# A trunk layer's output projection: its row multiply, its loads and its stores go to other engines, and one value tile moves behind the state space output

## The chip, the cores and the metric

The kernel runs on one core of a Trainium2 chip. The metric is the device time of one execution in microseconds (us); the time of a version is the median of its runs. TensorE (PE) does the matrix products, VectorE (DVE), ScalarE (ACT) and GpSimd (POOL) the elementwise work. SyncE (SP) only asks for transfers; ACT and POOL can ask for them too. Each engine works through its own list of instructions in order: an instruction that waits holds up all that stand behind it on that engine.

## The reference, cut to what matters

```python
h = rms_norm(x, mix_pre_g)
proj = h @ w_in                          # columns: u | q | k | v | f_logit
y_ssm = s5_mixer(u, ...)                 # scan over time, gelu(y), times sigmoid(g @ glu_w + glu_b)
y_fox = forgetting_attention(q, k, v, f_logit + fox_f_bias)      # 8 heads of 64
y_mix = concatenate([rms_norm(y_ssm, ssm_out_g), rms_norm(y_fox, fox_out_g)], -1)
x = x + rms_norm(y_mix @ w_out, mix_post_g)                      # the output projection
x = x + rms_norm(memory_cross_attention(rms_norm(x, xa_pre_g), ...), xa_post_g)
x = x + rms_norm(swiglu(rms_norm(x, ffn_pre_g), ...), ffn_post_g)
```

There are 1024 tokens of 1024 float32 values. `x1` below is x after the first of the three sums.

## The kernel before, in words

**Products.** A float32 product is made of three: each operand is split into a high part, rounded by an ACT copy (line 113), and the low rest, by a DVE subtraction (line 115, or 117 with a gain). `mm3` (lines 121 to 124) then multiplies high by high, high by low and low by high.

**The order of work.** The program is written by a framework that lists the instructions in the order in which the source makes them, and then plans the lists of the engines with a simulated clock. Of the instructions that are ready it takes the one with the best priority, which is the place in the source, moved ahead by 5000 places inside `tc.high_priority(offset=boost)`. Buffers come from pools with a fixed count for each tag; a tile that finds none free waits until all readers of an older tile are done. The tags that matter here: `t2` (3 buffers), `a` (2), `b` (2), `c` (3), `d` and `e` (1 each), `slab` (16), `raw` (2), `whl` (3). In PSUM there are four banks `g`, and during attention two double banks `s`, later four banks `x`.

**Where v and the state space output meet.** `in_proj` (line 869) ends with `V1_AT`: it makes that many tiles of the second half of v (`v1`, eight tiles of 24 products each, one `g` bank each), then takes one step of `ssm_out`, and so on:

```python
V1_AT = (3, 1, 1, 1, 1)
for n in V1_AT:
    step(v1, n)
    step(go)
drain(go)
```

A step of `ssm_out` (line 635) is either the four batches `b` of one half (lines 643 and 644, one `g` bank each, followed by a Gelu on ACT, line 645, into the slab `go`) or the transposes of one quarter (line 655). A v tile is copied from its bank by ACT (line 316) into a `t2` buffer, and POOL stores it (line 319). Before that the q and k tiles store their high parts from `t2` buffers too (line 297). What is left of `v1` is made by `fillers` (line 975), the side work that is spread over the steps of the attention `fox`.

**The output projection.** `out_ssm` (line 818) has stored the half result of the state space columns in `t1_d`. After attention the loop at line 1057 adds the half of the attention columns, tile by tile of 128 tokens, in the order 3, 4, 5, 6, 7, 0, 1, 2 (called n = 0 to 7 here). For a tile SP asks for x (tag `c`, line 1060), then for the half result `t` in two transfers (tags `a`, `a`, `b` in turn, line 1063). For each half of the columns PE makes 12 products into an `x` bank; DVE adds them, scaled by `r_f`, to `t` (line 1070); ACT squares two quarters (line 1072); POOL multiplies the half by the row `g_mp`, the gain `mix_post_g` for all partitions (line 1074). Then DVE sums the squares (1076), `rsqrt_mean` makes `r` with two small ACT and three small DVE instructions (lines 137 to 145), DVE forms x1 in the tile of x (line 1078), and for n = 0 to 4 POOL stores it (line 1082). The row `g_mp` lies in the one `d` buffer, which holds the sum of squares of the attention until line 815.

After each half of the columns the loop takes one step of `first_values`: the products of the cross-attention's values with its output weights for heads 0 and 1 (`value_weights`, line 1033, with its operand `vh` in a buffer of tag `b`, `e`, `b`, `e` for heads 0 to 3). Heads 2 and 3 and the `a` operands (`build_a(1)`) follow the loop.

Of the kernel before, what the change touches and what calls it, by code (L numbers as in the profile page):

```python
# [10 lines left out]
F32R = mybir.dt.float32r  # L11
BF16 = mybir.dt.bfloat16
AF = mybir.ActivationFunctionType
ALU = mybir.AluOpType
# [3 lines left out]
P = 128  # L18
# [16 lines left out]
MAGIC = 12582912.0  # L35
RATE = 1.02
HP = 16 * (L - 1)
V1_AT = (3, 1, 1, 1, 1)
HID = ("11", "12", "22", "S1", "S2", "S3", "S4")
EVB = 13  # L40
OPB = 10
# [11 lines left out]
def layer(ctx: ExitStack, tc: tile.TileContext, a, out):  # L53
    nc = tc.nc
    dve, act, pool, pe, sp = nc.vector, nc.scalar, nc.gpsimd, nc.tensor, nc.sync
# [13 lines left out]
    def slab(shape, dt=F32R):  # L69
        return slabp.tile(shape, dt, name="slab", tag="slab")  # L70
# [13 lines left out]
    def sm(n, name):  # L84
        return small.tile([P, n], F32, name=name, tag=name)
# [26 lines left out]
    def split(hi, lo, src, mul=None, lo_eng=None):  # L112
        first = act.activation(out=hi, in_=src, func=AF.Copy, scale=1.0 if mul is None else mul)  # L113
        if mul is None:
            (lo_eng or dve).tensor_tensor(out=lo, in0=src, in1=hi.bitcast(F32), op=ALU.subtract)  # L115
        else:
            dve.scalar_tensor_tensor(out=lo, in0=src, scalar=mul, in1=hi.bitcast(F32),
                                     op0=ALU.mult, op1=ALU.subtract)
        return first

    def mm3(ps, lh, ll, rh, rl, first, last):
        pe.matmul(ps, lh, rh, start=first, stop=False)  # L122
        pe.matmul(ps, lh, rl, start=False, stop=False)  # L123
        pe.matmul(ps, ll, rh, start=False, stop=last)  # L124
# [23 lines left out]
    boost = 5000  # L148
    stA, stB, stC = pool, pool, pool
# [4 lines left out]
    def load_w(src, shape, first=0, stage=None):  # L154
        w = tt(stage, [P, D]) if stage else raw([P, D])
        hl = whl([P, 2, D])
        if not first:
            sp.dma_start(out=w, in_=src)
        for cs in (slice(0, first), slice(first, D)):
            if cs.start < cs.stop:  # L160
                if first:
                    sp.dma_start(out=w[:, cs], in_=src[:, cs])
                with tc.high_priority(offset=boost):
                    split(hl[:, 0, cs], hl[:, 1, cs], w[:, cs])
        v = hl.rearrange("p t (a b) -> p t a b", b=shape)
        return v[:, 0], v[:, 1]
# [16 lines left out]
    t1_d = dram.tile([L, NC, D], F32, name="t1_d")  # L183
    kv_d = dram.tile([16, P, 256], F32, name="kv_d")
    x1_d = dram.tile([NT, P, D], F32, name="x1_d")
# [9 lines left out]
    def tt(tag, shape=None, dt=F32):  # L195
        return t4.tile(shape or [P, S], dt, name=tag, tag=tag, bufs=BUFS[tag])

    def t2t(shape, dt=F32):
        return tt("t2", shape, dt)
# [435 lines left out]
    def ssm_out():  # L635
        U, T, SS, mo = ssm_made
        for s_ in range(2):
            go = slab([P, 2, L, P], F32)
            with tc.high_priority(offset=boost):
                for b in range(4):  # L640
                    ps = g_ps([P, 4, NC])
                    for g in range(4):
                        pe.matmul(ps[:, g], U[s_][:, 4 * b + g], T[s_][:, 4 * b + g], start=True, stop=False)
                        pe.matmul(ps[:, g], SS[s_][:, 4 * b + g], mo[s_][:, 4 * b + g], start=False, stop=True)
                    g_ = act.activation(out=go[:, b // 2].rearrange("c j (g i) -> c g j i", i=16)[:, 4 * (b % 2):4 * (b % 2) + 4],
                                        in_=ps.rearrange("c g (j i) -> c g j i", i=16), func=AF.Gelu_apprx_tanh)
                    if (s_, b) == (0, 3):
                        last.append(g_)
            yield
            for ft in range(2):  # L650
                hl = slab([P, 2, S])
                for b in range(2):
                    tp = g_ps([P, 4, NC])
                    for j in range(4):
                        pe.transpose(tp[:, j], go[:, ft, 4 * b + j], ident)
                    cs = slice(512 * b, 512 * b + 512)
                    split(hl[:, 0, cs], hl[:, 1, cs], tp.rearrange("p j c -> p (j c)"))
                gl.append(hl)
                yield
# [192 lines left out]
    def step(g, n=1):  # L852
        for _ in range(n):
            if next(g, "end") == "end":
                return
# [13 lines left out]
    def in_proj():  # L869
# [11 lines left out]
        go = ssm_out()  # L881
        for n in V1_AT:
            step(v1, n)
# [61 lines left out]
    def gain_row(i, tag):  # L945
        g = tt(tag)
        sp.dma_start(out=g, in_=a["post_g"][i:i + 1, :].broadcast_to([P, D]))
        return g
# [71 lines left out]
    def x_ps(shape):  # L1020
        return psx.tile(shape, F32, name="x", tag="x")

    wo = []
    for i in range(4):
        w = raw([P, D])
# [1 line left out]
        hl = slab([P, 2, D])  # L1027
        split(hl[:, 0], hl[:, 1], w)
        wo.append(hl)
    g_mp = gain_row(0, "d")  # L1030
    VW = {}

    def value_weights(h):
        vr = t2t([P, 2, 256])
        sp.dma_start(out=vr, in_=kv_d[8 + 2 * h:8 + 2 * h + 2].rearrange("d p m -> p d m"))
        vh = tt("bebe"[h], [P, 2, 2, 256], F32R)
        split(vh[:, 0], vh[:, 1], vr)
        wo_ = [load_w(a["wo"][2 * h + d], 512) for d in range(2)]
        for mt in range(2):
            VW[2 * h + mt] = slab([P, 2, D])  # L1040
        for c in range(2):
            tiles = [(mt, (x_ps if h == 3 else g_ps)([P, 512])) for mt in range(2)]
            for d in range(2):
                for mt, ps in tiles:
                    ms = slice(mt * P, mt * P + P)
                    mm3(ps, vh[:, 0, d, ms], vh[:, 1, d, ms], wo_[d][0][:, c], wo_[d][1][:, c], d == 0, d == 1)
                    yield
            for mt, ps in tiles:
                split(VW[2 * h + mt][:, 0, c * 512:c * 512 + 512], VW[2 * h + mt][:, 1, c * 512:c * 512 + 512], ps)

    def first_values():
        for h in range(2):
            yield from value_weights(h)
# [2 lines left out]
    kept = {}  # L1056
    for n, j in enumerate((3, 4, 5, 6, 7, 0, 1, 2)):
        ts = slice(j * P, (j + 1) * P)
        xt = tt("c")
        sp.dma_start(out=xt, in_=a["x"][ts, :])  # L1060
        t = tt("aab"[n % 3])
        for i in range(2):
            sp.dma_start(out=t[64 * i:64 * i + 64], in_=t1_d.rearrange("j (k s) d -> s k j d", s=16)[2 * j + i])
        ss4, ss, r = sm(4, "ss4"), sm(1, "ss"), sm(1, "r")
        for h in range(2):
            hs = slice(h * 512, h * 512 + 512)
            ps = x_ps([P, 512])
            for k in range(4):
                mm3(ps, yf[k][:, 0, ts], yf[k][:, 1, ts], wo[k][:, 0, hs], wo[k][:, 1, hs], k == 0, k == 3)
            dve.scalar_tensor_tensor(out=t[:, hs], in0=ps, scalar=r_f[:, j:j + 1], in1=t[:, hs], op0=ALU.mult, op1=ALU.add)  # L1070
            for q in range(2 * h, 2 * h + 2):
                act.activation(out=tt("yt", [P, 256]), in_=t[:, q * 256:q * 256 + 256], func=AF.Square,
                               accum_out=ss4[:, q:q + 1])
            pool.tensor_tensor(out=t[:, hs], in0=t[:, hs], in1=g_mp[:, hs], op=ALU.mult)
            step(between)
        dve.tensor_reduce(out=ss, in_=ss4, op=ALU.add, axis=mybir.AxisListType.X)
        rsqrt_mean(r, ss, D)
        dve.scalar_tensor_tensor(out=xt, in0=t, scalar=r, in1=xt, op0=ALU.mult, op1=ALU.add)
        if j < 3:
            kept[j] = xt  # L1080
        else:
            stC.dma_start(out=x1_d[j], in_=xt)


    drain(between)
# [144 lines left out]

    keys = build_a(1)
    drain(value_weights(2))
    step(keys, KT // 2)
    xa_prep(0)
    drain(value_weights(3))
    xa_turn(0)
    drain(keys)
# [391 lines left out]
```

## Time and profile before

| | us |
|---|---|
| median of 3 runs | 1414.27 (1410.5, 1414.27, 1419.89) |
| the profiled execution: its own time | 1414.33 |
| its span, first to last instruction | 1412.5 |
| PE busy in the span | 1381.8 |
| DVE busy | 951.9 |
| ACT busy | 652.3 |
| POOL busy | 379.7 |

1.83 us of the profiled execution lie outside its span. Attention ends and the output projection begins at about 490 us of the span; the loop of line 1057 ends at about 558 us. Busy times overlap. A PE row's duration overlaps with that of its successor, so the distance between starts tells the pace: about 0.23 us for a product of 512 columns and 0.12 us for one of 256 at full clock, twice that at half clock.

### The profile page before, as it was taken

The numbers are of one execution on the slowest core, as the hardware profiler recorded it, in microseconds if no ns is written. First come the engines' busy times: TensorE is split into PE (matmuls) and PEld (weight loads), VectorE is DVE, ScalarE is ACT, GpSimd is POOL, SyncE is SP. The second block draws the span as 40 slices with busy tenths as digits, with TensorE's granted clock in tenths as the row PEclk, the third lists the DMA queues.
The fourth block names the chain that finished last, engine by engine and source line by source line (L and its number), as shares of the span: only waits on it lengthen the run. The fifth ranks groups of instructions, "written<-read, shape, count | busy, mean of one in ns | idle before, by whom it ended". The sixth has DMA issues, their size and how long they took to land.

```text
span 1412.5 us, 20273 instructions
## 1 busy us (share of the span) xinstructions
PE 1381.8 (98%) x7353; PEld 1163.3 (82%) x7353; DVE 951.9 (67%) x1719; ACT 652.3 (46%) x1289; POOL 379.7 (27%) x430
## 2 busy tenths in 40 slices
PE   9999989999999899999999999999999999999997
PEld 7889889789889677888888788888888888888886
DVE  8949944857567668545467777877776676655566
ACT  7383345766566546433344533333333334544351
POOL 0011110011211043001021367676766661000021
PEclk9999999999999999999999999999999999999999
DMA  6235665267663665024467345554444447955544
GB/s 217 91 108 163 201 220 138 69 200 213 183 180 113 175 194 186 27 75 152 161 202 257 97 176 193 178 187 161 145 158 154 165 150 236 357 196 194 179 164 164
DMA packets 104501, 239.45 MB, mean 170 GB/s; under 512 B 11464, under 2 KB 40136, under 8 KB 104272
## 3 DMA queue, kind: packets, MB, share of 16 engines
q1 hardware_dynamic: 85872, 176.24, 40.0%
q0 software_dynamic: 18528, 61.91, 12.3%
q8 instruction: 58, 0.95, 0.3%
q14 instruction: 43, 0.35, 0.1%
HBM read 169.43 MB, written 77.33 MB: 175 GB/s over the span
## 4 chain that ended last, share of the span: by engine, by line
PE 84%; DVE 7%; issue 3%; DMA 3%; ACT 2%; POOL 0%; SPq 0%; DVEq 0%; ACTq 0%; POOLq 0%
PE x L1294 17%; PE g L1294 13%; PE x L1557 7%; PE g L1557 7%; PE g L122 7%; PE g L124 7%; PE g L123 7%; PE x L123 2%; PE x L124 2%; PE g L758 2%; PE x L122 2%; PE g L772 2%; PE s L730 1%; PE s L731 1%; DMA a<-t_d 1%
## 5 line engine op out<-in xcount | busy, mean ns | idle before, releaser
L1294 PE MATMUL x<-slab,op 128*128 128x512 f32 x984 | 233.2, 389 | 0.5 <-DVE op L115 0.5
L1294 PEld LDWEIGHTS x<-slab,op 128*128 128x128 f32 x984 | 184.7, 188 | 39.2 <-DVE op L115 1.0
L1294 PE MATMUL g<-slab,op 128*128 128x512 f32 x744 | 178.7, 389 | 0.0
L115 DVE TENSOR_TENSOR slab<-slab 128x1024 fp32r<-128x1024 f32 (+2 forms) x92 | 110.2, 1207 | 86.4 <-ACT slab L113 85.2
L1294 PEld LDWEIGHTS g<-slab,op 128*128 128x128 f32 x744 | 139.7, 188 | 29.0
L122 PE MATMUL g<-slab,whl 128*128 128x512 f32 (+1 forms) x416 | 151.4, 364 | 0.8 <-ACT slab L485 0.4
L124 PE MATMUL g<-slab,whl 128*128 128x512 f32 (+1 forms) x416 | 148.7, 358 | 0.0
L123 PE MATMUL g<-slab,whl 128*128 128x512 f32 (+1 forms) x416 | 148.3, 357 | 0.0
L113 ACT ACTIVATE slab<-slab 128x1024 fp32r<-128x1024 f32 (+2 forms) x92 | 94.7, 1036 | 108.6 <-DMA slab<-hs_d 80.8
L1557 PE MATMUL g<-slab 128*128 128x512 f32 x462 | 126.6, 389 | 0.0
L1557 PE MATMUL x<-slab 128*128 128x512 f32 x462 | 126.6, 389 | 0.0
L1557 PEld LDWEIGHTS g<-slab 128*128 128x128 f32 x462 | 86.7, 188 | 18.0
L1557 PEld LDWEIGHTS x<-slab 128*128 128x128 f32 x462 | 86.7, 188 | 18.0
L115 DVE TENSOR_TENSOR op<-slab,op 128x512 fp32r<-128x512 f32 x80 | 84.6, 1068 | 11.5 <-ACT op L113 11.3
L1370 POOL TENSOR_TENSOR wt<-wt 128x256 f32<-128x256 f32 x88 | 83.1, 944 | 21.0 <-DMA wt<-in_w_down 17.4
L122 PE MATMUL g<-whl,slab 128*128 128x256 f32 (+2 forms) x288 | 86.8, 310 | 1.7 <-ACT yt L318 0.7
L122 PEld LDWEIGHTS g<-slab,whl 128*128 128x128 f32 x416 | 78.6, 189 | 12.0 <-ACT whl L113 0.6
L124 PEld LDWEIGHTS g<-slab,whl 128*128 128x128 f32 x416 | 78.4, 189 | 11.6 <-DVE whl L115 0.2
L123 PEld LDWEIGHTS g<-slab,whl 128*128 128x128 f32 x416 | 78.6, 189 | 10.6
L113 ACT ACTIVATE op<-slab 128x512 fp32r<-128x512 f32 x80 | 50.0, 628 | 79.9 <-PE g L1294 38.0
L124 PE MATMUL g<-whl,slab 128*128 128x256 f32 (+2 forms) x288 | 86.0, 299 | 0.0
L123 PE MATMUL g<-whl,slab 128*128 128x256 f32 (+2 forms) x288 | 85.7, 298 | 0.0
(397 smaller groups left out, 2890.3 us busy)
## 6 DMA issues: line engine op xcount, KB each, us to landing
hs_d<-ev POOLq DMA_DIRECT2D x77, 256.0 KB, 2.6
slab<-hs_d SPq DMA_DIRECT2D x35, 512.0 KB
wt<-in_w_down SPq DMA_DIRECT2D x44, 256.0 KB
wt_d<-wt POOLq DMA_DIRECT2D x22, 512.0 KB, 5.1
slab<-in_w_gate SPq DMA_DIRECT2D x20, 512.0 KB
slab<-in_w_up SPq DMA_DIRECT2D x20, 512.0 KB
slab<-wt_d SPq DMA_DIRECT2D x20, 512.0 KB
wd_d<-in_w_down SPq DMA_DIRECT2D x33, 256.0 KB
```

What stands on the lines that cost most here:

```text
L113: first = act.activation(out=hi, in_=src, func=AF.Copy, scale=1.0 if mul is None else mul)
L115: (lo_eng or dve).tensor_tensor(out=lo, in0=src, in1=hi.bitcast(F32), op=ALU.subtract)
L122: pe.matmul(ps, lh, rh, start=first, stop=False)
L123: pe.matmul(ps, lh, rl, start=False, stop=False)
L124: pe.matmul(ps, ll, rh, start=False, stop=last)
L730: pe.matmul(ps[:, c0:c1], qt, ka[:, 0, c0:c1], start=True, stop=False)
L731: pe.matmul(ps[:, c0:c1], qt, ka[:, 1, c0:c1], start=False, stop=not dg)
L758: pe.transpose(tp[:, k], sc[:, (k0 + k) * P:(k0 + k + 1) * P], ident)
L772: pe.matmul(yp[hh * 64:hh * 64 + 64, c0:], w, pts[2 * hp + hh, qc][:, k, c0:], start=k == 0, stop=k == nk - 1, tile_position=(0, 64 * hh))
L1294: pe.matmul(ps, x[:, k], y[:, k], start=first and k + n == 0, stop=k == 3 and n == 2, skip_group_check=not first)
L1370: pool.tensor_tensor(out=o, in0=x, in1=y, op=ALU.subtract)
L1557: pe.matmul(banks[n][j], xo[:, u, js], wo[:, v], start=ends[0] and k == 0, stop=ends[1] and k == 2, skip_group_check=onto is not None)
```

## The change: what it does

- `V1_AT` begins with 2 instead of 3: six instead of seven v tiles are made between the steps of `ssm_out`, and two instead of one are left to the fillers.
- The row `g_mp` is loaded into tag `e`, ahead of the four weights of the projection, instead of into `d` behind them. The operand `vh` of head 1 goes into `d` instead of `e`.
- The half results `t` are asked for ahead of x, at high priority.
- The row multiply of line 1074 is on DVE instead of POOL.
- The five x1 stores are asked for by ACT instead of POOL.

```diff
-V1_AT = (3, 1, 1, 1, 1)
+V1_AT = (2, 1, 1, 1, 1)
...
+    g_mp = gain_row(0, "e")
     wo = []
     for i in range(4):
...
-    g_mp = gain_row(0, "d")
...
-        vh = tt("bebe"[h], [P, 2, 2, 256], F32R)
+        vh = tt("bdbe"[h], [P, 2, 2, 256], F32R)
...
     for n, j in enumerate((3, 4, 5, 6, 7, 0, 1, 2)):
         ts = slice(j * P, (j + 1) * P)
+        t = tt("aab"[n % 3])
+        for i in range(2):
+            with tc.high_priority(offset=boost):
+                sp.dma_start(out=t[64 * i:64 * i + 64], in_=t1_d.rearrange("j (k s) d -> s k j d", s=16)[2 * j + i])
         xt = tt("c")
         sp.dma_start(out=xt, in_=a["x"][ts, :])
-        t = tt("aab"[n % 3])
-        for i in range(2):
-            sp.dma_start(out=t[64 * i:64 * i + 64], in_=t1_d.rearrange("j (k s) d -> s k j d", s=16)[2 * j + i])
...
-            pool.tensor_tensor(out=t[:, hs], in0=t[:, hs], in1=g_mp[:, hs], op=ALU.mult)
+            dve.tensor_tensor(out=t[:, hs], in0=t[:, hs], in1=g_mp[:, hs], op=ALU.mult)
...
         if j < 3:
             kept[j] = xt
         else:
-            stC.dma_start(out=x1_d[j], in_=xt)
+            act.dma_start(out=x1_d[j], in_=xt)
```

## The prediction

> **What bounds the kernel now.** I read the page's busy line and its chain first, to see which engine's idle time is worth anything.
>
> ```profile
> span 1412.5 us, 20273 instructions
> PE 1381.8 (98%) x7353; PEld 1163.3 (82%) x7353; DVE 951.9 (67%) x1719; ACT 652.3 (46%) x1289; POOL 379.7 (27%) x430
> PE 84%; DVE 7%; issue 3%; DMA 3%; ACT 2%; POOL 0%; SPq 0%; DVEq 0%; ACTq 0%; POOLq 0%
> ```
>
> PE is busy in 98% of the span and makes 84% of the chain; POOL has no share worth naming. The change takes no product away, so it can win only where PE waits or runs at half clock, and lose only by making such places. Before the rows below I went through PE's list in order of time, for waits in the two places that the diff touches, and then through the busy time by stretches:
>
> ```profile
> 190.00:200.00 10.00, 6.67 (x53) 6.47 (x52) 1.87 (x3) 2.59 (x4) 2.31 (x5) 0.87 1.00 332
> 200.00:210.00 10.00, 8.97 (x58) 8.58 (x57) 0.00 (x0) 3.82 (x6) 0.54 (x1) 0.79 0.50 161
> 501.60:558.00 56.40, 51.63 (x225) 40.93 (x224) 45.84 (x76) 30.79 (x104) 26.94 (x21) 0.97 0.65 206
> 540.00:560.00 20.00, 17.10 (x82) 12.98 (x81) 18.78 (x33) 14.86 (x40) 5.79 (x4) 0.91 0.62 191
> ```
>
> Columns: the stretch, its length, busy time of PE, PE's weight loads, DVE, ACT, POOL, the granted clock, the DMA share, GB/s. Where v meets the state space output (190 to 210) PE is idle for 4.4 us, and the clock is 0.87 and 0.79: if its low value is half, that is 2.6 us up to 200 and 4.2 us after it. In the projection loop (501.6 to 558) PE is idle for 4.8 us, and DVE is nearly full at its end: 18.78 of 20 us.
>
> **The change part by part: the v tile.** PE's list, then ACT's, then one piece of the chain:
>
> ```profile
> 190.35 0.39 PE L643 MATMUL g<-slab 128*128 128x128 f32 x2
> 193.84 0.36 PE L123 MATMUL g<-whl,slab 128*128 128x256 f32 x1
> 198.60 0.80 PE L643 MATMUL g<-slab 128*128 128x128 f32 x2 [3.33 <-ACT t L316]
> 202.03 0.56 PE L124 MATMUL g<-whl,slab 128*128 128x256 f32 x1
> 205.36 0.49 PE L643 MATMUL g<-slab 128*128 128x128 f32 x2 [0.56 <-ACT t L316]
> 207.88 0.39 PE L122 MATMUL g<-whl,slab 128*128 128x256 f32 x1 [0.46 <-ACT slab L645]
> 210.86 0.38 PE L655 MATMUL g<-ident,slab 128*128 128x128 f32 x2
> ```
> ```profile
> 198.07 0.47 ACT L316 ACTIVATE t<-g,r_x 128x256 f32<-128x256 f32 x1 [5.92 <-DMA qk_d<-t]
> 207.23 1.09 ACT L645 ACTIVATE slab<-g 128x512 f32<-128x512 f32 x2 [0.62 <-PE g L643]
> ```
> ```profile
> 189.63 8.34 DMA qk_d<-t
> ```
>
> Two v tiles come ahead of 190.35, then two batches b of the state space output (3.49 us, so 1.75 each), a part of the third v tile, a wait of 3.33, the third batch, the rest of the tile, a wait, the fourth batch, a wait. The cause is banks. The first Gelu starts only behind the fourth batch (207.23): its slab is taken from 16, of which eight hold the inputs and eight the U, T, SS and mo that the batches read, so none is free before. The four batches thus need all four g banks at once. The second v tile's bank is given up by ACT's copy at 198.07, which waits for a t2 buffer, held by a q store that takes 8.34 us to land; the third v tile holds the bank that the fourth batch needs.
>
> With the third tile behind the batches, by the same rows: three batches without a gap, 190.35 + 3 x 1.75 = 195.6; then the same wait until 198.60 for the second tile's bank; the fourth batch at half clock like the third, 198.60 to 202.03 (3.43 us); the Gelu (0.6, by the 1.09 of two) frees a bank at about 202.7; the tile's 24 products cost 2.98 us (207.88 to 210.86) at full clock, and 1.5 us of them fall before 204.2 at half clock, which gives 0.75 us of work: done at 202.7 + 1.5 + 2.2 = 206.4. In before that point is 207.88. The gain is **1.5 us**. Bounds: 0, if the planner keeps its order, and 7.6 us, all that the stretch loses (17.53 us from 190.35 to 207.88 for 4 x 1.75 + 2.98 us of work); I take the value that the rows build up, since nothing in the diff touches the store.
>
> A rule that speaks to this: in the Trainium skill, TensorE: Matmul & The Clock Gate, Part 1, the clock falls to half only after an idle window of about 3.4 us. By it the new wait, 3.0 us, could leave the clock whole, which is the third rival. The trace does not agree: the row at 549.13 below follows a wait of 2.0 us and is at half clock.
>
> The tile that moves costs PE the same 2.98 us among the fillers, and all side work behind it comes one step later. I cost that at 0, since PE has work for every step; what covers it is that order alone, so I keep 3 us both ways.
>
> **The half results, the row, and the multiply.** First the waits of PE, and the transfers behind the one that counts:
>
> ```profile
> 521.08 0.39 PE L124 MATMUL g<-whl,e 128*128 128x512 f32 x1
> 523.34 0.50 PE L122 MATMUL x<-slab 128*128 128x512 f32 x1 [1.87 <-DVE a L1070]
> 549.13 0.80 PE L122 MATMUL g<-whl,b 128*128 128x512 f32 x1 [2.00 <-DVE slab L115]
> 552.60 0.50 PE L122 MATMUL g<-whl,b 128*128 128x512 f32 x1 [0.55 <-DVE slab L115]
> ```
> ```profile
> 514.89 7.52 DMA a<-t_d
> 532.69 7.37 DMA a<-t_d
> ```
> ```profile
> 499.95 0.38 SPq L947 DMA_DIRECT2D d<-in_post_g  x1
> 514.25 3.62 SPq L1063 DMA_DIRECT2D a<-t_d  x4
> 504.73 7.02 POOL L1074 TENSOR_TENSOR a<-a,d 128x512 f32<-128x512 f32 x4 [8.46 <-ACT yt L1072]
> 512.07 2.16 DVE L1078 SCALAR_TENSOR_TENSOR c<-a,r,c 128x1024 f32<-128x1024 f32 x1
> ```
>
> The wait at 523.34 is for an x bank, which line 1070 of n = 3 frees, which waits for its half result, landed at 522.4. That was asked for at 514.25, when line 1078 of n = 0 (512.07 + 2.16) gave its buffer back. POOL's first multiply started only at 504.73, after the row, asked for at 499.95, had come. Where the order of asking is changed, it is this buffer and not the x load that sets the time: being ahead of x is worth nothing by itself.
>
> Now the price of a multiply on DVE, and what POOL's work cost DVE:
>
> ```profile
> L1074 POOL TENSOR_TENSOR a<-a,d x12: 1280/1302/2282, 504.7 to 552.0; 128x512 f32<-128x512 f32 x12
> L689 DVE TENSOR_TENSOR d<-d,t 128x512 f32<-128x512 f32 x6 | 4.1, 685 | 0.0
> L1078 DVE SCALAR_TENSOR_TENSOR c<-a,r,c 128x1024 f32<-128x1024 f32 x6 | 8.6, 1426 | 0.4
> L1078 DVE SCALAR_TENSOR_TENSOR c<-b,r,c 128x1024 f32<-128x1024 f32 x2 | 2.6, 1280 | 0.1
> L141 DVE SCALAR_TENSOR_TENSOR rst<-rsy,rsv 128x1 f32<-128x1 f32 x9 | 4.8, 532 | 1.9 <-ACT rsy L138 1.9
> L145 DVE SCALAR_TENSOR_TENSOR r<-rst,rsy 128x1 f32<-128x1 f32 x8 | 1.3, 159 | 0.2
> L115 DVE TENSOR_TENSOR b<-t,b 128x512 fp32r<-128x512 f32 x2 | 2.0, 1020 | 0.7 <-ACT b L113 0.7
> ```
>
> 16 multiplies x 0.685 = 11.0 us more on DVE. Against that, DVE instructions with two inputs in SBUF run long in this loop: line 141 takes 0.532 on one column where line 145 takes 0.159 (9 x 0.37 = 3.4 us), line 1078 takes 1.426 where its b form takes 1.280 (6 x 0.15 = 0.9), line 115 takes 1.020 where line 689 takes 0.685 (2 x 0.34 = 0.7). That these 5.0 us are POOL's doing is inferred; bounds of what comes back are 0 and 5.0, and I take 5.0. DVE's net load is 45.84 + 11.0 - 5.0 = 51.8 of 56.4 us: it fits, with 4.6 us to spare.
>
> For n = 0 the line 1078 itself ran 0.9 us long, and the chain ahead of it holds one long line 141; two multiplies of its own, 1.4 us, come on DVE in the time in which ACT makes its squares. So its buffer comes back earlier by 0.9 to 0.9 + 2 x 0.37 + 1.4 us, the last where POOL's queue was what it waited for; the middle is 2 us, and the half result lands at 520.4. PE needs the bank at 521.08 + 0.23 = 521.3, and line 1070 takes 0.74: PE still waits for 0 to 0.5 us. The gain is **1.7 us**, with bounds 0 and 1.9.
>
> In the tail (540 to 560) DVE has 20 - 18.78 = 1.2 us free. Tiles n = 6 and 7 put 4 x 0.685 = 2.7 us there, and some 1.5 us of hold-ups go. The second reload (532.69) comes about 2 us earlier and so does PE. These come out even: I take **0** for the waits at 549.13 and 552.60, with bounds of +4.5 and -4.3, worked out under the rivals.
>
> The other edits: the vh of head 1 is now split when d is free, which in before is just ahead of the asking at 499.95; that moves a DVE instruction of 0.7 us and an ACT copy of the same size into the start of the loop. What covers it is that most of head 1's products come late there, 521.08 among them. Taken at 0, bounds -0.7 and +0.7. The row's load moves ahead of the weights' on SP, out of the time in which POOL waited for it: 0, but it then shares the DMA engines with those weights; by the 7.5 us in which two halves of t and their company land, a quarter of that, up to +1.9.
>
> ```profile
> L1082 POOL DMA_DIRECT2D x_d<-c x5: 534/595/607, 514.5 to 535.1; - x5
> ```
>
> No store asked for by ACT is in this trace; POOL's take 0.595, SP's loads 0.38, so five cost ACT 1.9 to 3.0 us, out of 56.4 - 30.79 = 25.6 us that it has free. ACT's squares and splits stand behind each, and behind its wait for line 1078 (1.28 us). Cover: that idle time. I take 0, with bounds 0 and +2.
>
> **The sum**, against the profiled execution's 1414.33, which stands 0.06 above the median: 1414.33 - 1.5 - 1.7 = **1411.1**, a gain of 0.2%.
>
> **The rivals.** *DVE becomes the bound, and the kernel is slower.* For it: 18.78 of 20 us. Against it: 4.6 us to spare in the whole loop. If the hold-ups do not come back, line 1078 of n = 0 is not earlier and the 1.7 us stay lost, the four multiplies of the tail go ahead of the splits that PE waits for (2.7 us more at 549.13), and the longer wait costs a further window at half clock. The row at 549.13 is in such a window, 0.80 where 521.08 has 0.39, and the clock of 0.91 in 540 to 560 prices it: 20 x 0.09 = 1.8 us. That is +2.7 + 1.8 - 1.5 = +3.0: 1417.3. It decides when the tail needs over 1.2 us more of DVE.
>
> *The tail's waits go.* If the reload comes 3 us or more earlier, DVE has done n = 6 before the splits of the values; then 2.00 + 0.55 us of waits and the 1.8 us of half clock go: -4.3, in all 1406.8. Against it: the multiplies lie in the same place.
>
> *The clock stays whole behind the v tiles' wait.* The fourth batch ends at 198.60 + 1.75 = 200.35, the Gelu at 201.0, the tile at 204.0: a gain of 3.9 instead of 1.5, in all 1408.7. Against it: 549.13.
>
> *The v order does nothing* (the planner puts the tile where it was, or another wait takes its place): 1414.33 - 1.7 = 1412.6.
>
> **How the numbers follow.** My forecast 0.40, DVE bound 0.18, tail cleared 0.14, whole clock 0.13, v order without effect 0.15. Each is uncertain by the 3 us of the shifted side work. The range takes the tail's case less those 3 us and some of the open bounds, 1402, and the slow case with 2 us more, 1419. Faster by over 1%, about what a measurement of this kernel can tell from no change, would need 14.1 us, more than two cases together: 0.05. Slower by over 1%: 0.03. Within: 0.92.
>
> **What would show it.** Right: PE's list reads v, v, four batches, v, with one wait ahead of the fourth batch and the waits at 205.36 and 207.88 gone; POOL idle through the loop; line 141 near 0.16; the reload of n = 3 asked for by 512.5 and PE's wait on line 1070 under 0.5 us. Wrong: PE's wait on line 115 near 549 over 4 us; line 141 still near 0.5; half clock gone after 198; or a new wait of PE among the fillers between 235 and 500, since the planner lays the whole list anew.

## The result, and the profile after

The changed kernel takes 1418.22 us (median of 20 runs, 1415.91 to 1421.17), the kernel before 1413.24 us in the same comparison (20 runs, 1406.28 to 1419.89). The ratio is 1.0036 with an interval of 1.0024 to 1.0048: slower by 5 us. The forecast was 1411.1 us with a range of 1402 to 1419: the time lies just inside its upper end, and on the other side of no change.

The profiled execution took 1417.92 us. Its page, busy line and chain:

```profile
span 1416.2 us, 20245 instructions
PE 1382.7 (98%) x7353; PEld 1164.5 (82%) x7353; DVE 956.6 (68%) x1735; ACT 653.3 (46%) x1289; POOL 352.8 (25%) x409
...
PE 78%; DVE 10%; DMA 5%; issue 3%; ACT 3%; POOL 0%; SPq 0%; DVEq 0%; ACTq 0%; POOLq 0%
```

PE does the same work as before. Its share of the chain is 6 points lower; DVE (3), the transfers (2) and ACT (1) have them. The view by stretches, for the four stretches shown of before, and the last one cut in two:

```profile
190.00:200.00 10.00, 9.43 (x83) 9.23 (x82) 2.07 (x3) 4.06 (x6) 2.50 (x5) 1.00 1.02 333
200.00:210.00 10.00, 9.54 (x81) 9.35 (x81) 2.39 (x4) 5.06 (x10) 1.08 (x2) 1.00 0.51 174
501.60:558.00 56.40, 49.12 (x204) 39.68 (x203) 42.71 (x83) 29.10 (x98) 0.00 (x0) 0.92 0.63 192
540.00:560.00 20.00, 12.72 (x45) 9.79 (x45) 15.29 (x28) 12.22 (x33) 0.00 (x0) 0.74 0.52 159
...
540.00:550.00 10.00, 5.21 (x23) 3.96 (x22) 5.33 (x10) 3.75 (x14) 0.00 (x0) 0.98 0.82 241
550.00:560.00 10.00, 7.51 (x22) 5.82 (x23) 9.96 (x19) 8.47 (x21) 0.00 (x0) 0.51 0.23 77
```

Where v meets the state space output, PE is busy for 19.0 of 20 us at full clock (15.6 before). At the end of the loop it is busy for 12.7 of 20 us (17.1 before), and the clock is 0.74: 20 x 0.26 x 2 = 10.4 us at half clock, where before had 20 x 0.09 x 2 = 3.6. (That the low value is half is borne out by the 0.51 of 550 to 560, nearly all of which is slow.) And DVE, which was to be the tight engine there, is idle for almost half of 540 to 550 and full only behind it (9.96 of 10 us). So up to 550 it is not short of time; it waits for something, and then has to catch up.

PE's list of the changed kernel shows the places:

```profile
189.47 0.46 PE L643 MATMUL g<-slab 128*128 128x128 f32 x2 [1.50 <-DMA slab<-T_d]
...
194.82 0.36 PE L123 MATMUL g<-whl,slab 128*128 128x256 f32 x1
...
198.38 0.49 PE L643 MATMUL g<-slab 128*128 128x128 f32 x2 [0.57 <-ACT t L316]
200.90 0.39 PE L122 MATMUL g<-whl,slab 128*128 128x256 f32 x1 [0.46 <-ACT slab L645]
...
497.53 0.61 PE L237 MATMUL g<-ones,d 128*128 128x1 f32 x4 [2.77 <-POOL d L786]
...
550.24 0.79 PE L122 MATMUL g<-whl,b 128*128 128x512 f32 x1 [5.03 <-DVE rsv L139]
555.42 0.80 PE L122 MATMUL g<-whl,b 128*128 128x512 f32 x1 [2.25 <-DVE slab L115]
```

The waits of 2.00 and 0.55 us at 549 and 552.6 have become 5.03 and 2.25. (The row at 550.24 names line 139, the instruction that ran just behind the split which PE needs.) From the first transpose behind the loop (line 1090 before, 1091 after; 561.07 and 564.86) to the end, the two traces run with a nearly constant distance of 3.7 us: everything is lost ahead of it. At the last product of attention (line 772) the changed kernel is still 4.4 us ahead (485.42 against 489.78), so between there and the transpose it loses 8.1 us: 4.3 up to the last row of line 237 (the sums of squares of the attention, with the new wait of 2.77 us) and 3.8 from there on, in the loop and its tail.

What DVE waits for in the tail stands in its list. First three rows of before, then the same place after (line numbers are one higher):

```profile
530.75 1.28 DVE L1078 SCALAR_TENSOR_TENSOR c<-a,r,c 128x1024 f32<-128x1024 f32 x1
...
533.48 1.28 DVE L1078 SCALAR_TENSOR_TENSOR c<-a,r,c 128x1024 f32<-128x1024 f32 x1
...
540.17 0.75 DVE L1070 SCALAR_TENSOR_TENSOR a<-x,r_f,a 128x512 f32<-128x512 f32 x1 [0.92 <-DMA a<-t_d]
```
```profile
527.93 1.41 DVE L1071 SCALAR_TENSOR_TENSOR a<-x,r_f,a 128x512 f32<-128x512 f32 x2 [2.28 <-DMA a<-t_d]
...
530.51 0.68 DVE L1075 TENSOR_TENSOR a<-a,e 128x512 f32<-128x512 f32 x1
532.44 0.69 DVE L1075 TENSOR_TENSOR a<-a,e 128x512 f32<-128x512 f32 x1
...
533.11 0.74 DVE L1071 SCALAR_TENSOR_TENSOR b<-x,r_f,b 128x512 f32<-128x512 f32 x1
533.77 1.27 DVE L1079 SCALAR_TENSOR_TENSOR c<-a,r,c 128x1024 f32<-128x1024 f32 x1
...
536.73 1.29 DVE L1079 SCALAR_TENSOR_TENSOR c<-a,r,c 128x1024 f32<-128x1024 f32 x1
...
543.34 0.75 DVE L1071 SCALAR_TENSOR_TENSOR a<-x,r_f,a 128x512 f32<-128x512 f32 x1 [4.46 <-DMA a<-t_d]
...
548.84 0.75 DVE L1071 SCALAR_TENSOR_TENSOR a<-x,r_f,a 128x512 f32<-128x512 f32 x1 [1.21 <-DMA a<-t_d]
549.50 0.68 DVE L115 TENSOR_TENSOR slab<-g,slab 128x512 fp32r<-128x512 f32 x1
```

The last line of slice (tile) n = 3, the one that forms x1, starts at 533.77 instead of 530.75, that of n = 4 at 536.73 instead of 533.48. Counted from the loop's first add (500.10, before 501.63), the first is 33.7 us instead of 29.1. Both multiplies of n = 4 (530.51 and 532.44) and the first add of n = 5 now stand ahead of it in DVE's list, and the add at 527.93 that opens this group had waited 2.28 us for its own half result. The end of that line gives a buffer of tag `a` back, and SP asks for the next half result the moment it is free. SP's list of before, then of the changed kernel, and two pieces of the changed kernel's chain:

```profile
532.05 3.94 SPq L1063 DMA_DIRECT2D a<-t_d  x4
```
```profile
535.07 4.57 SPq L1062 DMA_DIRECT2D a<-t_d  x4
```
```profile
516.24 11.57 DMA a<-t_d
...
538.72 10.00 DMA a<-t_d
```

The half results of n = 6 and 7 are asked for from 535.07 on, 3.0 us later than before, the last piece at 538.72, and that one takes 10.00 us (the one that the add at 527.93 waited for took 11.57). DVE stands idle for them for 4.46 and 1.21 us, and behind the second of these adds stands the split at 549.50 that frees PE's bank.

### The profile page after: what moved, and what is told of

It is laid out like the page before. It is cut to its first block, busy times and chain, and to the rows that moved or that the text cites. A ratio compares the mean times of both kernels' runs of the same rounds, so it can differ in the third digit from the quotient of the medians.

```text
span 1416.2 us, 20245 instructions
## 1 busy us (share of the span) xinstructions
PE 1382.7 (98%) x7353; PEld 1164.5 (82%) x7353; DVE 956.6 (68%) x1735; ACT 653.3 (46%) x1289; POOL 352.8 (25%) x409
## 4 chain that ended last, share of the span: by engine, by line
PE 78%; DVE 10%; DMA 5%; issue 3%; ACT 3%; POOL 0%; SPq 0%; DVEq 0%; ACTq 0%; POOLq 0%
PE x L1295 17%; PE g L1295 13%; PE x L1558 7%; PE g L1558 7%; PE g L122 6%; PE g L124 6%; PE g L123 6%; PE x L124 2%; PE x L123 2%; PE x L122 2%; PE g L758 2%; PE g L772 2%; DMA a<-t_d 2%; DVE whl L115 1%; PE s L730 1%
## 5 line engine op out<-in xcount | busy, mean ns | idle before, releaser
L115 DVE TENSOR_TENSOR op<-slab,op 128x512 fp32r<-128x512 f32 x80 | 84.7, 1069 | 11.7 <-ACT op L113 11.3
L124 PEld LDWEIGHTS g<-slab,whl 128*128 128x128 f32 x416 | 78.4, 189 | 11.7 <-DVE whl L115 0.2
```

## The experiments

All ratios are against the kernel before, measured alongside; 1.001 is 1.4 us. Each kernel has 12 timed runs, the kernel before 35. An edit changes more than its own lines, since the planner then lays the lists of all engines anew.

**1. The v tiles alone** (the kernel before, with one line changed).

```diff
-V1_AT = (3, 1, 1, 1, 1)
+V1_AT = (2, 1, 1, 1, 1)
```

> The kernel before with V1_AT beginning with 2, nothing else of the change. Theory: the v step by itself wins about 4 us between 190 and 235 (no half clock near 198, fourth batch at about 198 instead of 205), but the end of attention is then held by the loads of the weights wo, which come when the raw buffers free; how much is left at 500 is open, so 1409 to 1413 against 1413. Rival A (the moved v tile is what makes the whole slower): 1416 to 1419, with a wait of PE between 235 and 300 that eats more than the 4 us.

Measured: 1411.47 us, ratio 1.0003 (0.9988 to 1.0017). The new order by itself is neither the loss nor a gain that can be seen.

**2. The projection's edits alone** (the changed kernel, with that line put back).

```diff
-V1_AT = (2, 1, 1, 1, 1)
+V1_AT = (3, 1, 1, 1, 1)
```

> The changed kernel with V1_AT back at 3: the edits of the output projection alone. Theory: the loss lies in the loop, its second reload comes later than before and PE waits near 550; +4 us, 1416 to 1419, with the wait of PE of 5 us near 550 there again. Rival A: 1412 to 1414, no such wait.

Measured: 1418.34 us, ratio 1.0038 (1.002 to 1.0055). The projection's edits alone lose as much as the whole change. The profile has the tail's waits again, 6.07 and 1.73 us. The execution profiled took 1410.66 us, though, the fastest of the twelve: it was 9.7 us ahead of before's trace at the last product of attention (480.05 against 489.78), and lost most of that lead up to the first transpose (557.20 against 561.07).

**3. The multiply back on POOL** (the changed kernel).

```diff
-            dve.tensor_tensor(out=t[:, hs], in0=t[:, hs], in1=g_mp[:, hs], op=ALU.mult)
+            pool.tensor_tensor(out=t[:, hs], in0=t[:, hs], in1=g_mp[:, hs], op=ALU.mult)
```

> The changed kernel with the row multiply back on POOL. Theory (the multiplies in DVE's list stand ahead of line 1079 and delay the buffer that the second reload needs): the reload of n = 6 is asked for by 532.5 instead of 535.1, PE's waits near 550 fall back to about 3 us, 1411 to 1414. Rival B (ACT's stores slow the transfers): unchanged, 1417 to 1419.

Measured: 1415.0 us, ratio 1.0023 (1.0011 to 1.0036). Between the two expectations: the reload of n = 6 is asked for at 530.24, as the theory had it, and PE's two waits are 2.00 and 1.82 us, but 3 us of the loss stay. The multiply is at most a part of it here.

**4. The stores back on POOL** (the changed kernel).

```diff
-            act.dma_start(out=x1_d[j], in_=xt)
+            stC.dma_start(out=x1_d[j], in_=xt)
```

> The changed kernel with the x1 stores back on POOL. Rival B (a store asked for by ACT shares the DMA engines in a way that makes the half results land in 8 to 11.6 us instead of 7.4): landing near 7.5 us again, DVE's wait for the half results 13.1 to about 7 us, 1412 to 1415. Theory of the multiply: landing and total unchanged, 1417 to 1419.

Measured: 1416.34 us, ratio 1.0034 (1.0023 to 1.0045), the changed kernel's own within the interval. DVE's waits for half results still come to 11.6 us (13.1 in the changed kernel). ACT's stores are not it.

**5. The buffer cycle** (the changed kernel; nothing but the order of the t buffers is changed).

```diff
-        t = tt("aab"[n % 3])
+        t = tt("aabaabba"[n])
```

> The changed kernel with its eight t buffers handed out in the order a a b a a b b a instead of a a b a a b a a, so that n=6 waits for n=2's buffer and n=7 for n=3's, each one slice earlier than now (now n=3's and n=4's); nothing is left out. Theory (the loss is the buffer cycle: with 16 more instructions in VectorE's list the last line of slices 3 and 4 ends 2.8 us later than before, so the half results of n=6 and n=7 are asked for and land late, and VectorE and then TensorE stand at the end of the loop): the loads of n=6 and n=7 are asked for by 531 and 535 us of the span, VectorE's 4.46 and 1.21 us before n=6 and n=7 go, TensorE's waits near 550 and 555 (5.19 and 2.65 us) fall to under 3 us together, and the time comes to 1411 to 1414 us where the kernel before gives 1411 to 1413 in the same job. Rival A (VectorE's own work in the tail is too much, whenever the half results come): the loads come earlier and the time stays at 1416 to 1419. Rival B (the loss stands ahead of the loop, in the wait of 2.93 us at 497.5): unchanged, 1416 to 1419, and that wait is still there while the tail's is gone.

Measured: 1412.42 us, ratio 1.001 (0.9994 to 1.0025): the theory's time, and all 16 multiplies are still on DVE. SP's list, DVE's and PE's of this kernel:

```profile
515.46 1.43 SPq L1062 DMA_DIRECT2D b<-t_d  x2
...
533.31 1.34 SPq L1062 DMA_DIRECT2D a<-t_d  x2
```
```profile
532.00 1.28 DVE L1079 SCALAR_TENSOR_TENSOR c<-a,r,c 128x1024 f32<-128x1024 f32 x1
...
536.83 0.75 DVE L1071 SCALAR_TENSOR_TENSOR b<-x,r_f,b 128x512 f32<-128x512 f32 x1
...
541.20 0.75 DVE L1071 SCALAR_TENSOR_TENSOR a<-x,r_f,a 128x512 f32<-128x512 f32 x1
```
```profile
540.73 0.50 PE L122 MATMUL g<-whl,b 128*128 128x512 f32 x1 [1.29 <-ACT b L113]
542.59 1.22 PE L124 MATMUL g<-whl,b 128*128 128x512 f32 x2 [0.68 <-DVE b L115]
550.12 0.39 PE L122 MATMUL g<-b,whl 128*128 128x256 f32 x1 [0.81 <-DVE slab L115]
```

The half result of n = 6 is asked for at 515.46 instead of 535.07, that of n = 7 at 533.31 instead of 538.1; n = 6 (in a buffer of tag `b` now; its first add stands at 536.83) and n = 7 (541.20) find theirs there, without a wait. In place of PE's waits of 5.03 and 2.25 us there are three of 1.29, 0.68 and 0.81. The last line of n = 3 is as late as in the changed kernel (532.00, 33.3 us behind the loop's first add at 498.68), but only n = 7 hangs on it now. Rival A, too much work for DVE whenever the data come, falls by the time: with the loads early, the same work holds PE up for less than 3 us, though DVE is busy through all of 540 to 550. The wait on line 237 is still there (3.01 us at 496.10), so rival B falls too.

**6. The row alone** (the kernel before; the row in `e` ahead of the weights, the second operand `vh` in `d`).

```diff
+    g_mp = gain_row(0, "e")
...
-    g_mp = gain_row(0, "d")
...
-        vh = tt("bebe"[h], [P, 2, 2, 256], F32R)
+        vh = tt("bdbe"[h], [P, 2, 2, 256], F32R)
```

> The kernel before with one edit, the gain row in tile e asked for ahead of the four w_out loads, and the value weights of head 1 in d. Theory (the part of the loss that stays when the multiply goes back to GpSimd, 3 us by ratio, comes from this edit: it moves the ones products of line 237 in TensorE's list, which then wait 2.9 to 3.5 us at the end of attention for ScalarE's and GpSimd's work behind a split of wo): TensorE waits 2 to 4 us on line 237 near 498 and the time is 1413 to 1416 us where the kernel before gives 1411 to 1413. Rival (the edit is free, as the prediction had it, and that part comes from the order of loads or the stores): within 1.5 us of the kernel before, and no such wait.

Measured: 1412.67 us, ratio 1.0005 (0.9988 to 1.0021), and no such wait in its profile (its execution, 1415.61 us, is the slowest of the twelve). The rival held.

**7. The multiply alone** (the kernel before).

```diff
-            pool.tensor_tensor(out=t[:, hs], in0=t[:, hs], in1=g_mp[:, hs], op=ALU.mult)
+            dve.tensor_tensor(out=t[:, hs], in0=t[:, hs], in1=g_mp[:, hs], op=ALU.mult)
```

> The kernel before with one edit, the 16 multiplies of line 1074 on VectorE instead of GpSimd. Theory (the multiply delays the last line of slices 3 and 4 by its place in VectorE's list, and with it the reload of the half results): the loads of n=6 and n=7 are asked for 2 to 4 us later than before's 532.3 and 534.8 against the loop's start, TensorE's waits in the tail grow by 2 to 5 us, and the time is 1413 to 1417 us. Rival (the multiply hurts only together with the moved row and loads): the time is that of the kernel before, within 1.5 us, and its waits at 549 and 552 stay near 2.2 and 1.0 us.

Measured: 1413.94 us, ratio 1.0019 (1.0002 to 1.0037). Slower by 2.7 us, as the theory had it, though the interval reaches down almost to no change, and with waits near those of run 2. PE's list and SP's of this kernel, whose loop starts 6.85 us earlier than before's:

```profile
543.29 0.79 PE L122 MATMUL g<-whl,b 128*128 128x512 f32 x1 [5.17 <-DVE slab L115]
547.95 0.79 PE L122 MATMUL g<-whl,b 128*128 128x512 f32 x1 [1.73 <-DVE slab L115]
```
```profile
526.97 1.23 SPq L1063 DMA_DIRECT2D a<-t_d  x2
533.04 0.33 SPq L1060 DMA_DIRECT2D c<-in_x  x1
533.47 1.22 SPq L1063 DMA_DIRECT2D a<-t_d  x2
```

526.97 + 6.85 = 533.8 and 533.47 + 6.85 = 540.3: the loads of n = 6 and 7 come 1.8 and 5.5 us later than before's 532.1 and 534.8. The first is a little under the theory's 2 to 4; the second stands behind an x load in SP's list, which was not expected.

The same measure for all traces with the old order of buffers: the load of n = 7 is asked for 38.0 to 39.4 us behind the loop's first add in the four kernels with the multiply on DVE (changed, runs 2, 4, 7), and 31.5 to 36.2 us behind it in the six with the multiply on POOL (before, runs 1, 3, 6, 8, 10).

**8. The order of asking alone** (the kernel before; `t` ahead of x at high priority).

```diff
+        t = tt("aab"[n % 3])
+        for i in range(2):
+            with tc.high_priority(offset=boost):
+                sp.dma_start(out=t[64 * i:64 * i + 64], in_=t1_d.rearrange("j (k s) d -> s k j d", s=16)[2 * j + i])
         xt = tt("c")
         sp.dma_start(out=xt, in_=a["x"][ts, :])
-        t = tt("aab"[n % 3])
-        for i in range(2):
-            sp.dma_start(out=t[64 * i:64 * i + 64], in_=t1_d.rearrange("j (k s) d -> s k j d", s=16)[2 * j + i])
```

> The kernel before with one edit, the half results asked for ahead of x and under the raised priority. Theory (the order of loads alone does nothing: the request waits for the buffer, not for SP's list): the loads of n=3 are asked for within 1 us of 514.25 and those of n=6 within 1 us of 532.3, and the time is that of the kernel before within 1.5 us. Rival (the x loads come later behind them and hold the last line of the slices, and with it the buffers and the stores): line 1078 of some slices waits for its x load, the time is 1413 to 1416 us. Rival in the other direction (the half results come earlier and VectorE's two waits of 6.6 us shrink): 1408 to 1410 us.

Measured: 1410.24 us, ratio 0.9992 (0.9973 to 1.0011): nothing that can be told from no change. Counted from the loop's first add (8.14 us earlier than before's), the loads of n = 3 and n = 6 are asked for 0.8 and 0.7 us earlier than in before, within the theory's 1 us.

**9. Both suspected causes away** (the changed kernel).

```diff
-V1_AT = (2, 1, 1, 1, 1)
+V1_AT = (3, 1, 1, 1, 1)
...
-        t = tt("aab"[n % 3])
+        t = tt("aabaabba"[n])
```

> The changed kernel with the eight t buffers in the order a a b a a b b a and the v tiles back in before's order. Theory (two separate losses after line 772's last product: the buffer cycle in the loop and tail, 3.8 us against before, and the wait of 3 us for line 237 at the end of attention, which only kernels with the new v order and the projection's edits together show): both are gone, TensorE waits under 1 us on line 237 near its last product and under 3 us in all in the tail, the stretch from the last L772 to the first L1091 is 69 to 72 us (71.3 before, 79.4 in the changed kernel, 73.0 with the new order of buffers alone), and the time is 1409 to 1412 us where the kernel before gives 1411 to 1413. Rival A (the wait on line 237 comes from the projection's edits alone): it stays at 2.5 us or more and the time is 1412 to 1415. Rival B (the new v order gives the 2 to 3 us that the front of the changed kernel seems to gain, so that taking it back costs them): 1413 to 1416.

Measured: 1410.95 us, ratio 1.0004 (0.999 to 1.0019). The time is the theory's: against run 2, the order of the buffers alone gives back 0.34% of 0.38%, with intervals that do not overlap. One detail missed; PE's list and a piece of the chain:

```profile
548.89 0.80 PE L122 MATMUL g<-whl,b 128*128 128x512 f32 x1 [3.76 <-DVE slab L115]
```
```profile
541.61 3.77 DMA t<-kv_d
```

One wait of 3.76 us is left in the tail, and what is late there now is the load of the next value operand, not the half result.

**10. Multiply on POOL, v tiles as before** (the changed kernel with the edit of run 3 and that of run 2).

```diff
-V1_AT = (2, 1, 1, 1, 1)
+V1_AT = (3, 1, 1, 1, 1)
...
-            dve.tensor_tensor(out=t[:, hs], in0=t[:, hs], in1=g_mp[:, hs], op=ALU.mult)
+            pool.tensor_tensor(out=t[:, hs], in0=t[:, hs], in1=g_mp[:, hs], op=ALU.mult)
```

> The changed kernel with the multiply back on GpSimd and the v tiles back in before's order: what is left of the change is the row in e, the half results asked ahead of x and the stores from ScalarE. Theory (with the multiply on GpSimd the loop and tail are before's, and without the new v order the wait on line 237 is gone): the stretch from the last L772 to the first L1091 is 71 to 73 us where the multiply on GpSimd with the new v order gave 75.8, and the time is that of the kernel before within 1.5 us. Rival (the 3 us that stayed when the multiply went back come from the stores or the row): 1413.5 to 1416 us.

Measured: 1411.91 us, ratio 1.0001 (0.9985 to 1.0017). Row, order of asking and ACT's stores together cost nothing that can be told from no change, and against run 2 the multiply alone makes up 0.37% of 0.38%, with intervals that do not overlap. The stretch was to be 71 to 73 us and is 74.0.

**11. Multiply on DVE and the new buffer order** (the kernel before).

```diff
-            pool.tensor_tensor(out=t[:, hs], in0=t[:, hs], in1=g_mp[:, hs], op=ALU.mult)
+            dve.tensor_tensor(out=t[:, hs], in0=t[:, hs], in1=g_mp[:, hs], op=ALU.mult)
...
-        t = tt("aab"[n % 3])
+        t = tt("aabaabba"[n])
```

> The kernel before with two edits, the multiplies on VectorE and the eight t buffers in the order a a b a a b b a. Theory (what a multiply on VectorE costs, 2.7 us when it was the only edit, is the late reload and not VectorE's work): VectorE's waits for the half results before n=6 and n=7 and TensorE's two waits in the tail (5.3 and 2.1 us with the multiply alone) fall to under 3 us together, and the time is 1409.5 to 1412.5 us where the kernel before gives 1411 to 1413. Rival (VectorE's 11 us of added work are the cost): the loads come earlier, the time stays 2 to 4 us above the kernel before.

Measured: 1412.13 us, ratio 1.0009 (0.9995 to 1.0023). The time lies in the theory's range, but the interval also holds run 7's 1.0019, so it is inconclusive. DVE has no wait left for the half results of n = 6 and 7; PE keeps one of 4.65 us on a split at 549.82, where, as in run 9, ACT waits for the load of the next value operand (4.2 us).

**12. The order of asking and the new buffer order** (the kernel before, with the edit of run 8 and this one; multiplies on POOL).

```diff
-        t = tt("aab"[n % 3])
+        t = tt("aabaabba"[n])
```

> The kernel before with two edits, the half results asked ahead of x under the raised priority, and the eight t buffers in the order a a b a a b b a; multiplies on GpSimd. Theory (in the kernel before too the tail's waits of 2.2 and 1.0 us and VectorE's 6.6 us of waits for half results come from the buffer cycle, so a shorter cycle gives 1 to 3 us): 1407.5 to 1410.5 us where the kernel before gives 1411 to 1413, TensorE waits under 2 us in all in the tail. Rival (before's tail is held by its other work, the splits and GpSimd's multiplies): within 1.5 us of the kernel before.

Measured: 1414.33 us, ratio 1.0023 (1.0005 to 1.0041). Both expectations missed: with the multiplies on POOL the new order of buffers makes the kernel slower. It is no gain of its own; it only heals what the multiply on DVE brings. Why it costs here was not tested. In the trace (the slowest of the twelve executions) the last lines of n = 4 and n = 5 wait 2.02 and 0.78 us for their x loads, which none does in before's, and PE waits 3.04 us at 552.30 and 1.98 at 557.21.

The stretch from the last product of attention (line 772) to the first transpose behind the loop, between starts in PE's list, beside the measured ratio:

| kernel | stretch, us | ratio to before |
|---|---|---|
| before | 71.3 | 1 |
| changed | 79.4 | 1.0036 |
| 1 v tiles alone | 73.5 | 1.0003 |
| 2 projection alone | 77.2 | 1.0038 |
| 3 multiply on POOL | 75.8 | 1.0023 |
| 4 stores on POOL | 79.5 | 1.0034 |
| 5 buffer order | 73.0 | 1.001 |
| 6 row alone | 74.5 | 1.0005 |
| 7 multiply alone | 74.0 | 1.0019 |
| 8 order of asking alone | 72.9 | 0.9992 |
| 9 buffer order, v as before | 71.6 | 1.0004 |
| 10 POOL, v as before | 74.0 | 1.0001 |
| 11 multiply alone, buffer order | 72.8 | 1.0009 |
| 12 order of asking, buffer order | 74.6 | 1.0023 |

The three slowest kernels have the three longest stretches. It is one execution each, and not always a typical one (those of runs 2 and 5 are the fastest of their twelve, those of runs 6 and 12 the slowest), so a difference of a microsecond or two says nothing.

**What stays open.** The multiply alone costs 2.7 us, with the other edits of the projection 5.4 (run 2, with intervals that overlap), though those alone cost nothing that shows (run 10): whether and which of them doubles it was not separated. And run 3 is 3 us slower than run 10, with intervals that overlap. The four kernels with the new v order and the projection's edits (changed, runs 3, 4, 5) wait 2.8 to 3.4 us on line 237 at the end of attention, for an addition on POOL; of the nine with the old order, six wait 1.5 to 2.6 us on line 772, a little earlier, and runs 2, 7 and 8 on neither; nor does run 1. That wait can't be worth much by itself: run 5 has it and stands at 1.001, run 9, the same kernel with the old order, is without it at 1.0004. Why the first reload's last piece took 11.57 us in the changed kernel (11.3 to 11.7 in runs 2, 4, 5, 9 and 11 too) is open as well. None of the kernels beats the kernel before by more than its interval.

## Why the prediction was wrong, point by point

**The tail: the step that failed.** "The second reload (532.69) comes about 2 us earlier and so does PE. These come out even." (The reload is the load of the half results of n = 6 and 7.) It came 3.0 us later, 535.07 instead of 532.05. The step carried over the gain of the first reload, whose working gave line 1078 two multiplies of its own slice and took away POOL's hold-ups. But the list of an in-order engine is written by the planner, and what matters is what stands ahead: for n = 0 the list of the changed kernel reads

```profile
509.06 1.28 DVE L1075 TENSOR_TENSOR a<-a,e 128x512 f32<-128x512 f32 x2
...
511.23 0.68 DVE L1075 TENSOR_TENSOR b<-b,e 128x512 f32<-128x512 f32 x1
...
512.22 1.28 DVE L1079 SCALAR_TENSOR_TENSOR c<-a,r,c 128x1024 f32<-128x1024 f32 x1
```

with both multiplies of n = 1 and one of n = 2 ahead of the last line of n = 0. So the first reload was asked for at 513.53 (by 512.5 forecast, 514.25 before), and its last piece landed only at 527.8 (516.24 + 11.57). Ahead of the last line of n = 3, which the second reload needs, there thus stood the wait of 2.28 us for that piece, both multiplies of n = 4 (1.4 us) and the first add of n = 5 (0.7). The two waits that the step took as unchanged grew from 2.55 to 7.28 us, and the half clock beside them from 3.6 to 10.4 us. Over loop and tail, from the last row of line 237 to the first transpose, the term taken at 0, with a bound of +4.5, measures +3.8 us (63.1 before, 67.0 after); that is net of the wait on line 1070, 1.87 us, which is gone, and it holds some 1.6 us for the half clock behind the wait on line 237 (clock 0.86 over 490 to 501.6). In run 5 the same stretch is 60.3 us.

**The rival "DVE becomes the bound, and the kernel is slower"** had the place, the waits (5.03 us against "2.7 us more" on 2.00) and nearly the time, 1417.3, but another cause; its sign, a wait on line 115 near 549 of over 4 us, came. It rested on hold-ups that do not come back and on a tail that needs over 1.2 us more of DVE. The hold-ups did come back, and DVE was idle for 4.7 of the 10 us from 540 to 550. A longer list made it late with handing a buffer back, and then it had to wait.

**The price of the multiply and the hold-ups: right.** The groups of the changed kernel's loop:

```profile
L1075 DVE TENSOR_TENSOR a<-a,e 128x512 f32<-128x512 f32 x12 | 8.1, 685 | 0.1
...
L1079 DVE SCALAR_TENSOR_TENSOR c<-a,r,c 128x1024 f32<-128x1024 f32 x6 | 7.7, 1281 | 0.1
...
L141 DVE SCALAR_TENSOR_TENSOR rst<-rsy,rsv 128x1 f32<-128x1 f32 x9 | 1.9, 215 | 0.0
L115 DVE TENSOR_TENSOR b<-t,b 128x512 fp32r<-128x512 f32 x2 | 1.4, 682 | 0.0
```

685 ns for a multiply as forecast, and line 141 falls from 532 to 215 ns, line 1079 from 1426 to 1281, line 115 from 1020 to 682: 4.4 of the 5.0 us came back. (The form of line 115 that reads a PSUM bank stays where it was, 680 and 684 ns.) Over the whole span DVE is busy for 4.7 us more, where the working had 11.0 - 5.0 = 6.0. That the hold-ups were POOL's doing, inferred in the working, fits. The Trainium skill, SBUF — State Buffer, "SBUF: two separate sides", says that a VectorE instruction with two SBUF inputs and a GpSimd one shut each other out for the whole instruction; these rows agree with it.

**The v tiles: another order, and worth nothing that shows.** PE's list was to read v, v, four batches, v. It reads v, three batches, v, the fourth batch, v: the planner put the batches ahead of the second tile too. The first of them then waits 1.50 us for the load of T (189.47; 1.4 to 2.2 us in all five kernels with the new order, in none with the old). Behind it the waits are down to 0.57 and 0.46 us, and the place that the working put at 206.4, against 207.88 in before, comes at 203.88: in these two traces 4.0 us are won, not 1.5. Yet run 1 gains nothing. The 3.33 us of before's profile were one execution's: in runs 7 and 8, where nothing ahead of the projection is changed, the first transposes start at

```profile
L655 PE MATMUL g<-ident,slab x32: 272/273/273, 206.7 to 225.9; 128*128 128x128 f32 x32
```
```profile
L655 PE MATMUL g<-ident,slab x32: 272/273/273, 204.3 to 223.4; 128*128 128x128 f32 x32
```

and in before's trace at 210.86. All nine traces with the old order have the same list here, and the wait at the third batch goes from 3.33 us (before) to none (runs 2 and 8). Their transposes start at 204.3 to 210.9, at 207.68 in the mean; those of the five with the new order at 203.5 to 206.3, at 204.35 in the mean. Of these 3.3 us, 2.98 are the tile that is now made later. The working took a wait for a store of 8.34 us as the rule; before's profile was the slowest of the nine at this place.

**PE's wait on line 1070: right for another reason.** It is gone, but the half result landed no earlier (the add of n = 3 starts at 522.36, 522.53 before). What covers the time is the planner's order: in before three products of the second value operand (tag `e`) stand ahead of the bank that PE waits for, in the changed kernel seventeen (tag `d`, 521.25 to 525.10). Run 2, with the same edits of the projection, still waits there, 1.04 us. So the gain of 1.7 us was not made by the earlier reload that the working built it on. And PE lost more than that ahead of the loop, in the wait of 2.77 us on line 237 at 497.53 and half clock behind it. That wait fits the sign "a new wait of PE among the fillers between 235 and 500".

**The row, `vh` and ACT's stores at 0: no cost that shows** (runs 6, 4 and 10; a store costs ACT's queue 0.33 us).

## What to carry to other kernels

Before work is moved to an in-order engine, ask not only whether its busy time fits, but which instruction of its list gives a buffer back, and what the new instructions put ahead of that one; the reload behind it then pays the whole transfer, here 10 us. Where a resource seems short, look whether the engine is idle just there: idle time with a wait on a transfer may mean a cycle of buffers, and another order of them may heal it without moving the work back, as in runs 5 and 9; where nothing is to be healed, the new order can cost (run 12). A wait that a single profile shows, above all one on a store's landing, should be seen in a second execution before it is counted as a gain.

## What the runs showed of the hardware

A short wait of PE may or may not bring half clock behind it. In the kernel before, 2.00 us at 549.13 did; in run 3, two waits of 2.00 and 1.82 us at 548.62 and 552.10 did not, and in run 5 two of 1.29 and 0.68 us that end at 540.73 and 542.59 did (the clock is 0.50 over 542.53 to 545.95). The stretches of run 3, then of run 5:

```profile
550.00:560.00 10.00, 6.83 (x46) 5.87 (x45) 9.13 (x20) 7.75 (x21) 1.28 (x1) 1.00 0.33 104
```
```profile
540.00:550.00 10.00, 7.88 (x24) 5.43 (x24) 10.00 (x21) 7.88 (x20) 0.00 (x0) 0.83 0.70 240
```

0.83 of 10 us is 3.4 us at half clock, and the changed kernel's 10.4 us in 540 to 560 are three times that. The Trainium skill, TensorE: Matmul & The Clock Gate, Part 1, tells of a free-running window of about 3.4 us, and of half clock after at least one idle window. The lengths agree with it; that equal waits differ would follow if a wait can fall into one window or across two, which no run here tests. That a whole window must be idle does not agree: 2.00 us were enough in before, and 1.97 us in two pieces in run 5. So the price of a wait can't be told from its length alone.
